# RWKV-7 units laid out by pairs of heads, with a new place for the projections of r and v, the adaLN steps and the output projection

## The chip, the cores and the metric

The kernel runs on one core of a Trainium2 chip. The metric is the device time of one execution in microseconds; of a kernel that is timed several times, the median counts. The core has engines with a queue each that run in order: TensorE (PE, with PEld for its weight loads), VectorE (DVE), ScalarE (ACT), GpSimd (POOL) and SyncE (SP), which issues most of the DMAs. Products go to PSUM, in banks that DVE and ACT read; everything else lies in SBUF, 128 partitions wide.

## What is computed

The reference is a trunk of two layers on 256 tokens of width 1024, in float32. Layer 0 is RWKV-7 time mixing and a dense SwiGLU; layer 1 is dilated attention and a mixture of experts. The change concerns the time mixing alone, 16 heads of 64 channels:

```python
def step(state, inp):
    r_t, w_t, k_t, v_t, a_t, b_t = inp
    sa = jnp.einsum('bhvk,bhk->bhv', state, a_t)
    state = state * w_t[:, :, None, :] + sa[..., None] * b_t[:, :, None, :] + v_t[..., None] * k_t[:, :, None, :]
    return state, jnp.einsum('bhvk,bhk->bhv', state, r_t)
...
_, y = lax.scan(step, s0, seq_in)
...
y = ((y - mu_y) * lax.rsqrt(var_y + LNX_EPS)).reshape(B, S, D) * lnx_g + lnx_b
bonus = (rh * kh * r_k).sum(-1, keepdims=True) * vh
y = y + bonus.reshape(B, S, D)
return (y * g).astype(h.dtype) @ w_out
...
def post_norm(t, y, l, j):
    gate = sub_mod[:, l, j, 2][:, None, :]
    return layer_norm(DEEPNORM_ALPHA * t + (1.0 + gate) * y, ln_g[l, j], ln_b[l, j])
```

r, k and v are projections of the modulated input, w, a and g come from small LoRA products, and the modulation rows (adaLN) are products of silu(c) with ada_w.

## The kernel before

**Units.** The scan is done in chunks of 64 tokens in matrix form. `unit(i, lane)` does four heads (256 channels, group `c_ = i // 2`) of 128 tokens (tile `t = i % 2`), which are two chunks `ch`. There are 8 units and 4 lanes; a lane has one PSUM tile (`psb0` to `psb3`, got with `lps`) and its own SBUF tiles, and unit i + 4 begins in the lane that is freed. A unit first makes the decayed vectors A, R (from a and r) and B, K; transposes them (ART and BKT); multiplies them to the masked scores SM; inverts a triangular matrix, E, in four doubling steps (`psb<-T,SM`, then `psb<-X,E` or, as the trace writes it, E,X) and two of 32x32; and then goes through its two chunks: products of SM with SV (which holds v and then the solved U), products of the state ST with ART, U times E, and the update of the state from SV and BKn. Y, the output of the chunk, is normalised, gated (g2t, w2t with lga, lgb) and transposed into `yg`.

**Layout.** The two halves of the partitions hold the two chunks, and the four heads lie one after the other in the free dimension. In the solve, `mm64` goes through heads and, inside, through the two halves, so neighbours alternate. The scores are made for `par = 0` and then for `par = 1`, each into the lane's tile. In the scan over chunks one half is at work at a time:

```python
for h in range(4):
    PE.matmul(ps[sl, h], E[sl, h], U[sl, h], start=True, stop=True)
```

BKn is built half by half on DVE. The update of the state is two 128x128 products, of which `pcm`, a mask with the decay in it that POOL writes, keeps the diagonal blocks.

**Order.** `spin` writes the instructions of the whole stage. Each task is a generator that yields the engine and the operands of its next step, or a condition. `spin` takes the step with the lowest pair of estimated start and order number, from a planner's clock that is part of the kernel. Units have the numbers 0 to 7. `rv_task` (number 100) makes the projections of r and v in 16 blocks of 24 matmuls; `ada_lane` (103) makes four adaLN rows of eight steps each, 512 KB of weights per step, with two buffers `rawa`; `pre_task` (104) makes the gate; `wo_task` (102) is the output projection, 96 matmuls from `yg` into the banks `mmb0` to `mmb3`, and begins when all of v, the gate and the rows are done; `pn_task` is the post-norm for each token tile, and `f0_task` the first piece of the SwiGLU. Numbers only decide between steps with the same estimate. Each engine then runs its list in order, so a step that waits holds what is listed behind it.

## Time and profile before

| | us |
|---|---|
| median of 3 runs | 1843.85 |
| lowest and highest | 1843.07, 1847.41 |
| profiled execution, own time | 1846.92 |
| profiled execution, span | 1845.2 |
| PE busy in the span | 1715.7 (93%) |
| DVE busy | 1497.0 (81%) |
| ACT busy | 1120.4 (61%) |
| POOL busy | 296.6 (16%) |

The profile is one execution; its span runs from the first to the last instruction, and its own time holds 1.7 us more. PE's share of busy time is an average over the whole trunk, most of which is the mixture of experts. The units lie between about 85 and 345 us. Below, a table by stretches gives busy time and granted clock there, groups of instructions give counts and means, and rows in order of time give the start of each run of equal instructions, its length, and in brackets how long the engine had been idle and for whom. A float32 matmul of the program shows as two in the trace.

### The profile page before, as it was taken

To read this page: it belongs to the slowest core of one execution; us is meant where nothing else is said; L and a number is where in the kernel's file an instruction comes from. 1 tells how busy PE (TensorE), PEld (TensorE's weight loads), DVE (VectorE), ACT (ScalarE), POOL (GpSimd) and SP (SyncE) were. 2 spreads that over 40 slices of the span, in tenths; PEclk is the share of its full clock that TensorE was granted. 3 is DMA by queue.
4 is the path that set the end of the run, shared out by engine and by line. 5 is a ranking of instruction groups with operands and counts; after the bars stand their busy time and mean duration, and the time that the engine had idled before them with its cause. 6 is when DMAs were issued, how large, how long until landed. Compare 5 with 4: busy or idle time off the path is not lost. (4 is left out here: it accounts for less than half of the span.)

```text
span 1845.2 us, 26366 instructions
## 1 busy us (share of the span) xinstructions
PE 1715.7 (93%) x9828; PEld 1368.3 (74%) x9828; DVE 1497.0 (81%) x2044; ACT 1120.4 (61%) x1447; POOL 296.6 (16%) x222
## 2 busy tenths in 40 slices
PE   6998998869998888979999999999999999999896
PEld 3676776558876666778888888888788787788674
DVE  2786786389886768579899898998888988988888
ACT  3443342236553656438777777877777777777674
POOL 0012222044532785250000000000000000000200
PEclk8998998889998999979999999999999999999998
DMA  9551153559894574568999999999999999999880
GB/s 330 155 160 30 54 164 116 150 189 357 296 354 151 194 256 154 195 230 293 334 352 368 357 349 380 348 360 332 345 368 340 352 345 349 352 344 359 311 320 24
DMA packets 213564, 498.94 MB, mean 270 GB/s; under 512 B 14634, under 2 KB 28818, under 8 KB 213428
## 3 DMA queue, kind: packets, MB, share of 16 engines
q1 hardware_dynamic: 212564, 494.03, 75.7%
q0 software_dynamic: 864, 3.15, 0.5%
q8 instruction: 79, 1.29, 0.3%
q14 instruction: 57, 0.47, 0.1%
HBM read 496.07 MB, written 1.06 MB: 269 GB/s over the span
## 5 line engine op out<-in xcount | busy, mean ns | idle before, releaser
L190 DVE TENSOR_TENSOR wlo<-raw,whi 128x1024 fp32r<-128x1024 f32 x800 | 991.6, 1277 | 138.0 <-ACT whi L190 123.7
L190 ACT CAST whi<-raw 128x1024 fp32r<-128x1024 f32 x808 | 823.9, 1048 | 291.9 <-PE mmb L190 221.2
L190 PE MATMUL mmb<-wlo,xeh 128*128 128x512 f32 x896 | 355.9, 397 | 5.9 <-DVE wlo L190 5.2
L190 PE MATMUL mmb<-whi,xeh 128*128 128x512 f32 x896 | 352.5, 394 | 0.0
L190 PE MATMUL mmb<-whi,xel 128*128 128x512 f32 x896 | 351.6, 392 | 0.0
L190 PEld LDWEIGHTS mmb<-wlo,xeh 128*128 128x128 f32 x896 | 168.4, 188 | 48.3 <-DVE wlo L190 14.9
L190 PEld LDWEIGHTS mmb<-whi,xeh 128*128 128x128 f32 x896 | 168.4, 188 | 34.2 <-ACT whi L190 0.2
L190 PEld LDWEIGHTS mmb<-whi,xel 128*128 128x128 f32 x896 | 168.4, 188 | 32.6
L190 PE MATMUL psb<-wlo,ah 128*128 128x512 f32 x448 | 176.7, 394 | 1.5 <-DVE wlo L190 1.5
L190 PE MATMUL psb<-whi,al 128*128 128x512 f32 x448 | 174.7, 390 | 0.0
L190 PE MATMUL psb<-whi,ah 128*128 128x512 f32 x448 | 161.8, 391 | 0.0
L190 POOL TENSOR_TENSOR macc<-macc,gate 128x1024 f32<-128x1024 f32 x2 | 5.7, 2889 | 924.8 <-ACT gate L190 924.8
L190 POOL TENSOR_TENSOR acc<-acc,raw 128x512 f32<-128x512 f32 (+1 forms) x62 | 128.2, 2082 | 74.2 <-DVE acc L190 42.9
L190 PEld LDWEIGHTS psb<-wlo,ah 128*128 128x128 f32 x448 | 84.1, 188 | 24.6 <-DVE wlo L190 6.2
L190 PEld LDWEIGHTS psb<-whi,ah 128*128 128x128 f32 x448 | 83.5, 188 | 18.8 <-ACT whi L190 1.6
L190 PEld LDWEIGHTS psb<-whi,al 128*128 128x128 f32 x448 | 84.2, 188 | 16.4
L190 PE MATMUL mmb<-whi,f_xl 128*128 128x512 f32 (+1 forms) x192 | 72.1, 375 | 1.1 <-DVE f_xl L190 1.1
L190 PE MATMUL mmb<-whi,f_xh 128*128 128x512 f32 (+1 forms) x192 | 72.7, 379 | 0.0
L190 PE MATMUL mmb<-wlo,f_xh 128*128 128x512 f32 (+1 forms) x192 | 72.0, 375 | 0.2 <-DVE wlo L190 0.2
L190 ACT CAST ah<-psb 128x512 fp32r<-128x512 f32 x56 | 32.6, 583 | 60.3 <-PE psb L190 60.2
L190 ACT ACTIVATE e_s<-mmb 128x512 f32<-128x512 f32 x56 | 33.5, 599 | 44.8 <-PE mmb L190 44.8
L190 DVE TENSOR_TENSOR e_s<-e_s,mmb 128x512 f32<-128x512 f32 x56 | 38.2, 683 | 22.5 <-PE mmb L190 22.2
(417 smaller groups left out, 2589.3 us busy)
## 6 DMA issues: line engine op xcount, KB each, us to landing
raw<-in_moe_w_gu_dram SPq DMA_DIRECT2D x192, 1024.0 KB, 6.6
raw<-in_moe_w_down_dram SPq DMA_DIRECT2D x83, 1024.0 KB, 6.1
raw<-in_moe_w_gu_dram SPq DMA_DIRECT2D x60, 512.0 KB, 7.0
raw<-in_moe_w_down_dram SPq DMA_DIRECT2D x56, 512.0 KB, 6.0
raw<-in_ada_w_dram SPq DMA_DIRECT2D x37, 512.0 KB, 5.3
rawa<-in_ada_w_dram SPq DMA_DIRECT2D x35, 512.0 KB, 4.2
raw<-in_ada_w_dram SPq DMA_DIRECT2D x15, 1024.0 KB, 7.8
raw<-in_ffn_w_gu_dram SPq DMA_DIRECT2D x21, 512.0 KB, 5.3
```

The lines of the kernel that those rows point to most:

```text
L190: return fn(*a, **kw)
```

## The change

- In the scan and the solve the halves of the partitions now hold pairs of heads (`hp`), and `ch * 2 + hh` lies in the free dimension; `each` and `products` go through both halves in turn.
- The scores of `par` 0 and 1 are issued in turn into two banks, the lane's and `mmb2`. A lock, `bank2`, lets one unit at a time into the second; the gate takes the same lock.
- B and K are built at full width (`Bf`, `Kf`, in the place of kQ) and transposed from there; BKn is filled by eight copies of 64x128 after the solve, and SV by four of 64x128 after one full memset.
- `pcm` is gone: POOL clears each new state, and DVE adds and scales the diagonal halves alone, at 64x128 each. The update of the state is four products of 64x64.
- `lgb` moves into a tile with zeros around it, and its product runs over 128 rows instead of 32.
- `rv_task` and `ada_lane` get the number 3.5; `ada_lane` takes its weight rows in pairs, both loaded before the eight matmuls of the two. `wo_task` waits in addition until all units have their masked scores (`sm_n`).
- Steps carry a hint on the shape, which has the weight zero in the planner (`SHP = 0`); the planner's estimates are otherwise as before.

```diff
-            for st in ada_pe(i, ada_raw, lambda: mmt(3), 256):
-                yield lambda: True
-                yield st
+            for q in range(0, 8, 2):
+                rws = [ada_raw(i, q + j) for j in range(2)]
+                yield PE, "128x32", rws[0], rws[1]
+                if q == 0:
+                    ps = mmt(3)
+                    PE.matmul(ps[:, 0:256], zero[:, 0:128], zero, start=True, stop=False)
+                for j in range(2):
+                    for g in range(4):
+                        PE.matmul(ps[g * 32:g * 32 + 32, 0:256], cs_act[:, q + j:q + j + 1].to_broadcast([128, 32]),
+                                  rws[j][:, g * 256:g * 256 + 256], start=False, stop=q + j == 7,
+                                  tile_position=(0, g * 32))
+            yield from ada_end(i, ps)
...
+        lgb.append(ringed("xh", 2, ap_.tile([128, S], F32, name="xh", bufs=2)))
+        yield GP,
+        GP.memset(lgb[0][:, 0:S], 0.0)
+        for dst, src in ((lga, psg), (lgb[0][96:128], psg2)):
...
+        yield V, ta, kkr
+        Bf, Kf = kkr, Q
+        V.scalar_tensor_tensor(Bf, ta, 1.0, kkr, op0=OP.add, op1=OP.mult)
+        yield V, k2, Q
+        V.tensor_tensor(Kf, k2, Q, op=OP.mult)
+
+
+        yield lambda: not bank2[0]
+        bank2[0] = 1
...
+        yield PE, "128x128", A, R, Bf, Kf
         ART = lt("ART", "ART", (128, 2, 2, 2, 64))
-        ps = lps((128, 2, 2, 2, 64))
+        BKT = lt("BKT", "BS", (128, 2, 2, 2, 64))
+        ps, psk = lps((128, 2, 2, 2, 64)), mmt(2, (128, 2, 2, 128))
...
-        yield V, kkr
-        BKn = lt("BKn", "BKn", (128, 2, 256))
-        halves(lambda sl, ch: V.scalar_tensor_tensor(BKn[sl, ch], ta[sl], 1.0, kkr[sl], op0=OP.add, op1=OP.mult))
...
+        for src, a in ((Bf, 0), (Kf, 1)):
+            for p in range(2):
+                PE.transpose(psk[:, p, a], src[:, p * 128:(p + 1) * 128], ident)
...
+        pss = [lps((128, 2, 2, 128)), mmt(2, (128, 2, 2, 128))]
+        for ch in range(2):
+            for pr in range(2):
+                for par in range(2):
+                    sl = slice(par * 64, par * 64 + 64)
+                    PE.matmul(pss[par][:, ch, pr], BKT[sl, pr, ch].rearrange("q a t -> q (a t)"),
+                              ART[sl, pr, ch].rearrange("q a t -> q (a t)"), start=True, stop=True)
...
-        for par in range(2):
-            sl = slice(par * 64, par * 64 + 64)
-            yield PE, BKT, ART
-            ps = lps((128, 2, 2, 128))
-            for ch in range(2):
-                for pr in range(2):
-                    PE.matmul(ps[:, ch, pr], BKT[sl, pr, ch, :], ART[sl, pr, ch].rearrange("q a t -> q (a t)"),
...
+        bank2[0] = 0
+        sm_n[0] += 1
...
+        def each():
+            for ch in range(2):
+                for hh in range(2):
+                    for hp in range(2):
+                        yield slice(hp * 64, hp * 64 + 64), ch, 2 * hp + hh, ch * 2 + hh
...
+        for ch in range(2):
+            for hp in range(2):
+                s_, cs_ = slice(ch * 64, ch * 64 + 64), slice(hp * 128, hp * 128 + 128)
+                for src, d in ((Bf, hp), (Kf, 1 - hp)):
+                    e = pick([SC, V], src)
+                    yield e, src
+                    (SC.copy if e is SC else V.tensor_copy)(BKn[d * 64:d * 64 + 64, ch, cs_], src[s_, cs_])
...
-        SC.copy(SV[64:128, 0], v_[0:64])
-        SC.copy(SV[0:64, 1], v_[64:128])
         yield GP,
-        GP.memset(SV[0:64, 0], 0.0)
-        GP.memset(SV[64:128, 1], 0.0)
+        GP.memset(SV.rearrange("p c n -> p (c n)"), 0.0)
+        for ch in range(2):
+            for hp in range(2):
+                s_, cs_ = slice(ch * 64, ch * 64 + 64), slice(hp * 128, hp * 128 + 128)
+                yield SC, v_, SV
+                SC.copy(SV[64 - hp * 64:128 - hp * 64, ch, cs_], v_[s_, cs_])
...
-        pcm = lt("pcm", "t34", (128, 2, 2, 128))
...
+        def products(ps, ch, a, st):
+
+            for hh in range(2):
+                for hp in range(2):
+                    h = 2 * hp + hh
+                    PE.matmul(ps[hp * 64:hp * 64 + 64, hh], SM[:, ch, h, a * 64:a * 64 + 64],
+                              SV[:, ch, h * 64:(h + 1) * 64], start=hh == 0, stop=st is None and hh == 1)
+            return ps
+
+        def with_state(ps, ch, a, st):
             for pr in range(2):
-                PE.matmul(ps[sl, 2 * pr:2 * pr + 2].rearrange("p h n -> p (h n)"), ART[:, pr, ch, a], st[:, pr],
-                          start=False, stop=pr == 1)
+                PE.matmul(ps[pr * 64:pr * 64 + 64].rearrange("p h n -> p (h n)"), ART[:, pr, ch, a], st[:, pr],
+                          start=False, stop=True)
...
+            for hh in range(2):
+                for hp in range(2):
+                    sl = slice(hp * 64, hp * 64 + 64)
+                    PE.matmul(ps[sl, hh], E[sl, ch * 2 + hh], U[sl, ch * 2 + hh], start=True, stop=True)
+            for hp in range(2):
+                sl = slice(hp * 64, hp * 64 + 64)
+                e = SC if hp else V
+                yield e, ps
+                (SC.copy if hp else V.tensor_copy)(SV[sl, ch, hp * 128:hp * 128 + 128],
...
+                ps2 = lps((128, 2, 64))
                 for pr in range(2):
-                    prs = slice(pr * 128, (pr + 1) * 128)
-                    PE.matmul(ps2[:, pr], BKn[:, ch, prs], SV[:, ch, prs], start=True, stop=True)
+                    for par in range(2):
+                        hsl = slice(pr * 128 + par * 64, pr * 128 + par * 64 + 64)
+                        PE.matmul(ps2[par * 64:par * 64 + 64, pr], BKn[:, ch, hsl], SV[:, ch, hsl], start=True,
+                                  stop=True)
                 yield V, ps2
-                sn = lt("ST", "t1", (128, 2, 128)) if ch == 0 else up.tile([128, 2, 128], F32, name=f"ST{c_ % 2}",
-                                                                                   bufs=1)
...
+                    cur = lt("Sc", "t34", (128, 2, 64))
+                    halves(lambda sl, par: V.tensor_tensor(cur[sl], ps2[sl], diag(st, sl, par), op=OP.add))
+                    yield V, cur
+                pc = PC[:, :, ch].unsqueeze(2)
+                halves(lambda sl, par: V.tensor_tensor(diag(sn, sl, par), cur[sl], pc[sl].to_broadcast([64, 2, 64]),
+                                                       op=OP.mult))
...
-            yield PE, hi, lo, xl, ps[0], ps[1]
+            yield 3.5, PE, hi, lo, xl, ps[0], ps[1]
...
-        yield lambda: len(vsb) == 8 and "gate" in pre and not ada_left[0]
+        yield lambda: len(vsb) == 8 and "gate" in pre and not ada_left[0] and sm_n[0] == 8
...
+        yield lambda: not bank2[0]
+        bank2[0] = 1
         yield from bcast_steps(2, o, lambda: mmt(2))
+        bank2[0] = 0
...
-                if isinstance(need[0], int):
+                if isinstance(need[0], (int, float)):
...
-                 (103, ada_lane(LANE)), (104, pre_task()), (105, pn_task(0)), (106, pn_task(1)),
+                 (3.5, ada_lane(LANE)), (104, pre_task()), (105, pn_task(0)), (106, pn_task(1)),
```

The order on PE where unit 3 ends and unit 4 begins; numbers tell buffers of one name apart, the figure in names such as T_4 is the unit, and mmb with x0h or x2h is a block of r or v. Before:

```order
L190 MATMUL psb_2422<-SV_3_2313,SM_3_1854 64x64 x4
L190 MATMUL psb_2422<-ST1_2050,ART_3_1399 64x128 x2
L190 MATMUL psb_2435<-sg_6_2429,cst2_112 128x256
L190 MATMUL psb_2440<-SV_3_2313,SM_3_1854 64x64 x4
L190 MATMUL psb_2440<-ST_3_2416,ART_3_1399 64x128 x2
L190 MATMUL psb_2453<-cst_79,sg_5_2139 128x128 x2
L190 MATMUL psb_2453<-cst_79,P_5_2176 128x128 x2
L190 MATMUL psb_2462<-T_4_2450,SM_4_2364 64x64 x8
L190 MATMUL psb_2475<-U_3_2318,E_3_1937 64x64 x4
L190 MATMUL mmb_2353<-whi_2207,x0h_254 128x256
```

And after:

```order
L191 MATMUL mmb_2613<-rawa_2569,cs_act_96 32x256 x4
L191 MATMUL mmb_2613<-rawa_2571,cs_act_96 32x256 x4
L191 MATMUL psb_2646<-U_3_2487,E_3_1764 64x64 x4
L191 MATMUL psb_2655<-cst_79,sg_4_2102 128x128 x2
L191 MATMUL psb_2655<-cst_79,P_4_2148 128x128 x2
L191 MATMUL mmb_2656<-cst_79,kQ_4_2086 128x128 x4
L191 MATMUL psb_2671<-SV_3_2457,SM_3_1655 64x64 x4
L191 MATMUL psb_2671<-ST_3_2489,ART_3_1618 64x128 x2
L191 MATMUL psb_2681<-w2t_265,lw_267 128x256
L191 MATMUL psb_2681<-a2t_266,la_268 128x256
L191 MATMUL psb_2695<-ART_4_2653,BKT_4_2654 128x128
L191 MATMUL mmb_2696<-ART_4_2653,BKT_4_2654 128x128
```

Before, unit 4 is in its solve while a block of r begins; after, unit 4's scores (ART_4, BKT_4) alternate between two tiles, all blocks of r and v stand ahead of this piece, and adaLN steps come in pairs.

The order on PE at the end of unit 7 (mmb with ygh or ygl is the output projection, cst with Y_7 the transposes of the unit's result). Before:

```order
L190 MATMUL mmb_3698<-rawa_3837,cs_act_96 32x256 x4
L190 MATMUL mmb_3698<-rawa_3860,cs_act_96 32x256 x4
L190 MATMUL mmb_3698<-cst_79,row_3892 128x128 x2
L190 MATMUL mmb_3901<-whi_2666,ygh_1125 128x512
L190 MATMUL mmb_3901<-wlo_2667,ygh_1125 128x512
L190 MATMUL mmb_3901<-whi_2666,ygl_1126 128x512
L190 MATMUL psb_3910<-g2t_868,lga_269 128x256
L190 MATMUL psb_3910<-w2t_265,lw_267 128x256
L190 MATMUL mmb_3902<-whi_2666,ygh_1125 128x512
L190 MATMUL mmb_3902<-wlo_2667,ygh_1125 128x512
L190 MATMUL mmb_3902<-whi_2666,ygl_1126 128x512
L190 MATMUL psb_3917<-cst_79,Y_7_3763 128x128 x2
```

And after:

```order
L191 MATMUL psb_4114<-U_7_4019,E_7_3695 64x64 x4
L191 MATMUL mmb_3690<-whi_4048,ygh_1087 128x512
L191 MATMUL mmb_3690<-wlo_4049,ygh_1087 128x512
L191 MATMUL mmb_3690<-whi_4048,ygl_1088 128x512
L191 MATMUL mmb_3690<-whi_4071,ygh_1087 128x512
L191 MATMUL mmb_3690<-wlo_4072,ygh_1087 128x512
L191 MATMUL mmb_3690<-whi_4071,ygl_1088 128x512
L191 MATMUL psb_4128<-SV_7_4013,SM_7_3615 64x64 x4
L191 MATMUL psb_4128<-ST_7_4021,ART_7_3589 64x128 x2
L191 MATMUL psb_4168<-g2t_864,lga_269 128x256
L191 MATMUL psb_4168<-w2t_265,xh_775 128x256
L191 MATMUL psb_4178<-cst_79,Y_7_4020 128x128 x2
```

Before, the projection begins behind the last adaLN step, with six of its matmuls ahead of Y_7; after, it lies between the links of unit 7, and 84 of its 96 matmuls stand ahead of Y_7.

The order on ACT from the last products of unit 7's solve to its first chunk. Before:

```order
L190 COPY X_7_3660<-psb_3646 128x256
L190 COPY row_3677<-mmb_3253 128x256
L190 ACTIVATE ysq_6_3679<-Y_6_3520 128x256
L190 COPY X_7_3702<-psb_3703 32x4x32 x2
L190 COPY gate1_3699<-mmb_3725 128x512
L190 COPY SV_7_3757<-vsb1_2781 64x256 x2
L190 CAST ygh_1125<-psb_3774 128x2x128
L190 COPY U_7_3762<-psb_3768 64x256
L190 COPY SV_7_3757<-psb_3788 64x256
L190 COPY gate1_3699<-mmb_3800 128x512
```

And after:

```order
L191 COPY X_7_3934<-psb_3916 128x256
L191 CAST whi_3957<-raw_3880 128x1024
L191 COPY X_7_3962<-psb_3963 32x4x32 x2
L191 COPY BKn_7_3694<-kQ_7_2886 64x128 x8
L191 COPY SV_7_4013<-vsb1_2820 64x128 x4
L191 CAST ygh_1087<-psb_4032 128x2x128
L191 COPY U_7_4019<-psb_4027 128x128
L191 CAST whi_4048<-raw_3929 128x1024
L191 COPY SV_7_4013<-psb_4040 64x128
L191 CAST whi_4071<-raw_3982 128x1024
```

Before, two copies fill SV_7 ahead of U_7; after, eight to BKn_7 and four to SV_7 stand there, and casts of the projection's weights (whi) lie between the unit's copies.

## Rows read from the trace of the kernel before

**Rows 1.** Stretches: length, busy us of the engines (instructions), granted clock, DMA, GB/s.

```profile
85.00:159.00 74.00, 67.10 (x837) 55.80 (x835) 61.36 (x174) 31.23 (x77) 12.31 (x21) 1.00 0.41 123
159.00:204.00 45.00, 40.25 (x416) 31.62 (x416) 27.09 (x101) 13.94 (x38) 9.83 (x16) 0.74 0.03 8
204.00:250.00 46.00, 43.04 (x506) 35.91 (x504) 36.79 (x100) 19.63 (x47) 13.61 (x21) 1.00 0.43 136
250.00:295.00 45.00, 39.66 (x581) 29.10 (x577) 37.68 (x133) 16.38 (x47) 10.02 (x18) 1.00 0.41 129
295.00:339.00 44.00, 36.52 (x439) 24.81 (x439) 17.41 (x62) 11.68 (x31) 6.95 (x12) 0.81 0.49 144
```

**Rows 2.** Groups on PE, 85 to 339: shape, count, busy us, mean, idle before.

```profile
L190 PE MATMUL psb<-SV,SM 128*64 128x64 f32 x256 | 23.4, 240 | 4.8 <-DVE ST L190 2.2 <-DVE E L190 1.0 <-DVE bon L190 0.9
L190 PE MATMUL mmb<-rawa,cs_act 128*32 128x256 f32 x256 | 21.8, 419 | 4.8 <-DMA rawa<-in_ada_w_dram 4.8
...
L190 PE MATMUL psb<-ART,BKT 64*128 64x128 f32 x128 | 18.4, 284 | 3.1 <-DVE yna L190 2.3 <-ACT BKT L190 0.7
L190 PE MATMUL psb<-ST,ART 128*64 128x128 f32 x96 | 15.2, 283 | 0.0
...
L190 PE MATMUL psb<-U,E 64*64 64x64 f32 x128 | 11.9, 240 | 0.0
L190 PE MATMUL psb<-SV,BKn 128*128 128x128 f32 x48 | 10.0, 339 | 0.0
```

**Rows 3.** PE in order of time, three places: start, us, what, count.

```profile
121.71 1.16 PE L190 MATMUL psb<-ART,BKT 64*128 64x128 f32 x8
122.80 0.68 PE L190 MATMUL psb<-E,X 64*64 64x64 f32 x16
...
150.83 0.68 PE L190 MATMUL psb<-E,X 64*64 64x64 f32 x16
151.44 0.71 PE L190 MATMUL psb<-SV,BKn 128*128 128x128 f32 x4
152.08 0.68 PE L190 MATMUL psb<-E,X 64*64 64x64 f32 x16
152.84 0.68 PE L190 MATMUL psb<-SV,SM 128*64 128x64 f32 x8
153.36 0.60 PE L190 MATMUL psb<-ST,ART 128*64 128x128 f32 x4
153.89 0.82 PE L190 MATMUL psb<-T,SM 32*32 32x32 f32 x24
...
322.92 0.67 PE L190 MATMUL psb<-U,E 64*64 64x64 f32 x8
323.53 0.64 PE L190 MATMUL mmb<-rawa,cs_act 128*32 128x256 f32 x8
324.10 1.16 PE L190 MATMUL mmb<-cst,mod 128*128 128x128 f32 x8
```

**Rows 4.** Groups on ACT and DVE, 85 to 345.

```profile
L190 ACT COPY SV<-vsb 64x256 f32<-64x256 f32 x16 | 6.4, 403 | 0.4
...
L190 ACT COPY X<-psb 32x128 f32<-32x128 f32 x16 | 4.1, 258 | 9.4 <-PE psb L190 9.1
...
L190 DVE SCALAR_TENSOR_TENSOR BKn<-ta,kQ 64x256 f32<-64x256 f32 x16 | 6.8, 423 | 0.1
```

**Rows 5.** PE in order of time, end of the stage.

```profile
334.54 0.64 PE L190 MATMUL mmb<-rawa,cs_act 128*32 128x256 f32 x8 [2.16 <-DMA rawa<-in_ada_w_dram]
...
339.10 0.78 PE L190 MATMUL mmb<-whi,ygh 128*128 128x512 f32 x1
...
344.11 0.63 PE L190 MATMUL psb<-cst,Y 128*128 128x128 f32 x2
...
378.27 1.11 PE L190 MATMUL psb<-cst,u 128*128 128x128 f32 x4 [9.43 <-DVE u L190]
```

**Rows 6.** The page's DMA issues: count, KB each, median us to landing.

```profile
rawa<-in_ada_w_dram SPq DMA_DIRECT2D x35, 512.0 KB, 4.2
```

More of the change, by code (lines that the diff above doesn't have):

```diff
@@ L1039, in unit @@
             SC.copy(X, ps)
-            yield PE, X
+            yield PE, "64x64", X
             ps = lps((128, 4, 64))
-            mm64(ps, lambda sl, ch, h: X[sl, h], lambda sl, ch, h: E[sl, h])
+            for sl, ch, h, j in each():
+                PE.matmul(ps[sl, j], X[sl, j], E[sl, j], start=True, stop=True)
             yield V, ps
@@ L1101, in unit @@
-            first = t == 0 and ch == 0
-            yield PE, SV
-            ps = lps((128, 4, 64))
-            for h in range(4):
-                PE.matmul(ps[sl, h], SM[:, ch, h, 0:64], SV[:, ch, h * 64:(h + 1) * 64], start=h == 0,
-                          stop=first and h == 3)
+            first, final = t == 0 and ch == 0, t == 1 and ch == 1
+            if not final:
+                sn = lt("ST", "t1", (128, 2, 128)) if ch == 0 else up.tile([128, 2, 128], F32, name=f"ST{c_ % 2}",
+                                                                           bufs=1)
+                yield GP,
+                GP.memset(sn.rearrange("p r n -> p (r n)"), 0.0)
@@ L1110, in unit @@
                 st = ST[c_]
-                yield PE, st
-                with_state(ps, sl, ch, 0, st)
-            yield SC, ps
-            SC.copy(U[sl], ps[sl])
-            yield PE, U
-            ps = lps((128, 4, 64))
-            for h in range(4):
-                PE.matmul(ps[sl, h], E[sl, h], U[sl, h], start=True, stop=True)
-            yield SC, ps
-            SC.copy(h4(SV[sl, ch]), ps[sl])
-            if not (t == 1 and ch == 1):
-                yield PE, SV
-                ps2 = lps((128, 2, 128))
+            yield PE, "128x64", SV
@@ L1134, in unit @@
                 ST[c_] = sn
                 ST_n[c_] = t * 2 + ch + 1
-            yield PE, SV
-            ps = lps((128, 4, 64))
-            for h in range(4):
-                PE.matmul(ps[sl, h], SM[:, ch, h, 64:128], SV[:, ch, h * 64:(h + 1) * 64], start=h == 0,
-                          stop=first and h == 3)
+            yield PE, "128x64", SV
+            ps = lps((128, 2, 64))
+            products(ps, ch, 1, st)
             if not first:
-                with_state(ps, sl, ch, 1, st)
@@ L1143, in unit @@
[L1143 to L1144 removed]
+                with_state(ps, ch, 1, st)
+            for hp in range(2):
+                yield SC, ps
+                SC.copy(Y[ch * 64:ch * 64 + 64, 2 * hp:2 * hp + 2], ps[hp * 64:hp * 64 + 64])
         yield GP, v_, bon
```

114 lines of the change are left out of this document (60 added, 54 removed).

## The prediction

> **What bounds the kernel now.** I read the stage table first [rows 1], because the change touches only the RWKV-7 stage and the start of the output projection, about 85 to 380 us of a span of 1845.2 us. The reader is to see three things. PE is busy 67.10 of 74 us, then 40.25 of 45, 43.04 of 46, 39.66 of 45 and 36.52 of 44: it is the fullest engine, but no stretch is solid, and DVE has 61.36 of 74 us in the first, so a faster PE would soon meet DVE there. The granted clock is 1.00 in three stretches and only 0.74 and 0.81 in the second and the last, where almost nothing but units runs; those two are mixtures of 1.2 and 2.4 GHz. In the last stretch ACT (11.68) and DVE (17.41) are nearly idle and PE still has gaps: what ends last there is the chain of the last two units. Then I read the groups on PE by shape, for counts [rows 2], and the order of time, for the price from one run's start to the next [rows 3]; the mean of a matmul in a group is longer than its price, since matmuls overlap. Last I read the end of the stage [rows 5]: the first matmul of the output projection stands at 339.10, the last unit's transposes (Y) at 344.11, and the first product of the post-norm (u) at 378.27, after 9.43 us without any PE work. So 34.2 us lie between the last unit and the next stage, in which the projection has no company.
>
> **PE work taken away.** A matmul of the program is two in the trace, so a run of four is x8. The new layout issues neighbours that lie in different halves of the array, where the old one issued them in the same half.
> - Masked scores (ART,BKT): 128 in the groups are 16 runs, 1.09 us each (121.71 to 122.80) [rows 2, 3], 17.4 us. Alternating halves, at best half: -8.7. That a row half runs beside the other is shown for 64-column products: 16 of E,X, which alternate, take 0.61 us (150.83 to 151.44), as long as 8 of U,E, which don't (322.92 to 323.53).
> - Products (SV,SM): 256 are 32 runs of 0.52 us, 16.6 us; they now alternate between column halves: -8.3. Column groups are shown by rawa: 8 matmuls of 256 columns in four groups take 0.57 us (323.53 to 324.10), 71 ns each, where one of 128 columns with the state takes 0.53/4 = 133 ns.
> - With the state (ST,ART): 96 are 24 runs of 0.53 us (153.36 to 153.89), 12.7 us, also in column halves: -6.4.
> - U,E: 16 runs of 0.61 us, now like E,X: -4.9.
> - State update (SV,BKn): 48 are 12 runs of 0.64 us (151.44 to 152.08). Four 64-wide ones in column halves cost half a run of SV,SM, 0.26: 12 x 0.38 = -4.6; without any company they cost 0.52, -1.4.
> The sum is -32.9 us if every pair shares the array and -1.4 if none does; I take -31, because both kinds of sharing stand in the rows, though not with 128 columns. The transposes of B and K read the full-width tiles and are as many as before, and the LoRA product over 128 rows instead of 32 has as many columns: nothing for both.
> Half of the 31 falls on units 0 to 3. PE is busy 107.35 of 119 us up to 204, but DVE has 61.36 of 74 in the first stretch, which covers part: I take **-12** of 15.5 (bounds -5 and -15.5). On units 4 to 7 PE is busy 119.2 of 135 us, with the projections of r and v as filler that now goes ahead (the order at unit 4: before, a block of r follows unit 4's first solve product; after, all blocks stand ahead of its scores). These four blocks change place, not amount: nothing in the sum. With less filler the chain counts, not PE: **-6** of 15.5 (bounds 0 and -14).
>
> **The end of the stage.** In the order of before, the projection stands behind the last adaLN row, and only that lies ahead of the last unit's tail. After, it begins behind unit 7's scores, and 84 of its 96 matmuls stand ahead of unit 7's Y. The last 12 cost about 3 us by a pace of (368.85 - 344.11)/(96 - 6) = 0.27 us, where 368.85 is 378.27 less the idle 9.43 [rows 5], and 6 stand ahead of Y in the order of before. The two banks of the first token tile are complete before Y, so the post-norm's first part doesn't wait for the last unit. Y to u becomes 3 + 9.4 = 12.4 us instead of 34.2: **-22**. The price is that 84 matmuls, 19 to 24 us of PE, go between the links of units 6 and 7. Their cover is the idle 7.48 us of 295 to 339, some 8 us freed there by the layout, and the place of 13 adaLN steps (13 x 0.57 = 7.4 us) that leave this stretch. That is 23 us: just enough, so this term can lose up to all of it (bounds -28, with a shorter 9.4, and 0). Its weights' casts go to ACT and DVE, busy 11.68 and 17.41 of 44 us there: nothing.
>
> **What is added.**
> - adaLN in pairs. Both rows are now loaded after the pair before has freed both buffers, and PE, which runs in order, waits with all units' products behind it when the second is late. A load takes 4.2 us [rows 6]. Before, all single steps together waited 4.8 us, the longest 2.16 us [rows 2, 5]. Some 10 pairs follow unit 4's start. Between -5 (the late steps vanish since they come earlier) and +21 (all ten wait 2.1 us) I take **+5**, nearer to the rows of single steps, since most of those didn't wait.
> - Narrow copies on a unit's path. After the solve ACT has eight copies of 64x128 to BKn and four to SV, where it had two of 64x256. Twelve at 258 ns (the nearest small copy, 32x128) are 3.1 us, at 403 ns (64x256) 4.8 us, less 0.8 [rows 4]. The third excerpt shows them in a row ahead of unit 7's U. Per unit +2.3 to +4.0, two generations of units in a lane, other lanes' work fills part: **+4** (bounds 0 and +8). On DVE the four 64x256 steps of 423 ns that built BKn per unit become two of full width: a small gain off the path.
> - The guard on the second bank of the scores: a unit that reaches its scores waits for the other's masks. Only two or three units are ever near; in the sum of the next point.
> - Clock and queues. Without the filler, 204 to 295 may be granted as 159 to 204 was (0.74 instead of 1.00). If PE were the bound, 82.7 us of work would grow by a third; with the chain as bound it costs only the links' own PE time. I take **+4** (bounds 0 and +12).
> Sum: -12 - 6 - 22 + 5 + 4 + 4 = **-27 us**. The profiled execution's own time is 1846.92 us, 1.72 over its span, so 1819.9 on its scale; the median is 3.07 us lower, so 1816.8, **1817 us**. What follows the stage moves as a whole: from 400 us on I assume that it keeps its length.
>
> **A rule against the rows.** E,X alternates between row halves and writes one bank, and still runs twice as fast as U,E [rows 3]. The Trainium skill, TensorEngine Tiling (Array Packing), Restrictions and Gotchas, says that different row tiles cannot access the same PSUM bank at once. By that rule U,E would gain nothing (the scores go to two banks) and the sum would be 2 to 3 us smaller; the trace's 0.61 us for 16 speaks against it.
>
> **Rivals.**
> 1. *The freed PE time isn't felt* (0.17): the chain of a unit bounds everywhere, or halves don't share the array with wide operands. Against it stand 107.35 of 119 us of PE. Then -18 becomes -4: -13, **1831 us**. The rule above, as a case of its own in which U,E alone keeps its length, has 0.02 and gives **1820 us**.
> 2. *The projection isn't hidden* (0.10), so the change doesn't do what its order says: the 84 matmuls fall on PE when units 6 and 7 need it, or their weights come late, and Y moves by what is saved behind it. For it: the cover was just enough. -22 becomes -3: -8, **1836 us**.
> 3. *All of it is felt* (0.19): PE gives -25, the projection -26, and the additions cost 8: -43, **1801 us**. For it: PE is the fullest engine in all five stretches.
> 4. *Slower* (0.06): the pairs. When each of ten pairs stalls PE for a whole load, 4.2 us, all lanes stop together: +42 instead of +5 gives +10, **1854 us**. It decides from 3.2 us per pair on (then the sum is zero). Against it: the longest wait of a step is 2.16 us, and the planner spaces the pairs.
>
> **How the numbers follow.** The forecast, 1807 to 1827 us, has 0.46. The range of 1799 to 1838 us takes in rivals 1, 2 and more than half of 3, and leaves out rival 4 and the far end of 3. About 0.3% (5.5 us) is what a measurement can tell from no change. Faster: 0.46 + 0.17 + 0.02 + 0.19 and a third of rival 2, 0.87; the same: most of the rest of 2, 0.06; slower: rival 4 and its neighbourhood, 0.07.
>
> **What would show it.** In the profile after: runs of eight scores near 1.1 us that were two of 1.09; products in 0.26; unit 4's scores with no r or v product behind them; u about 12 us behind unit 7's Y, and Y itself some 5 us earlier than 344.11. It is wrong if the alternating runs keep their length (rival 1), if Y comes later than 360 with projection matmuls between the links (rival 2), if PE shows waits of 3 us and more for rawa (rival 4), or if the stages behind 400 us change in length.

## The result, and the profile after

The changed kernel takes 1827.76 us (median of 4 runs, 1827.28 to 1830.45) where the kernel before takes 1844.26 (4 runs); the ratio is 0.9900, with a 95% interval of 0.9881 to 0.9918. The forecast was 1817 us, in a range of 1799 to 1838: the sign and the range held, the gain was 16.5 us instead of 27.

Stretches of the profile after, as in [rows 1]: length, busy us of PE, PEld, DVE, ACT, POOL (instructions), granted clock, DMA share, GB/s.

```profile
85.00:159.00 74.00, 65.21 (x925) 55.45 (x926) 59.01 (x179) 34.83 (x99) 10.51 (x17) 0.99 0.45 137
159.00:204.00 45.00, 41.83 (x571) 34.64 (x569) 26.82 (x78) 20.03 (x54) 7.28 (x13) 0.94 0.40 136
204.00:250.00 46.00, 36.87 (x458) 23.44 (x454) 42.14 (x154) 19.08 (x61) 9.57 (x13) 0.89 0.51 171
250.00:295.00 45.00, 36.76 (x599) 27.47 (x598) 31.90 (x112) 23.38 (x80) 7.80 (x15) 0.87 0.32 106
295.00:339.00 44.00, 38.65 (x383) 26.74 (x382) 28.14 (x80) 18.62 (x44) 5.75 (x8) 0.97 0.29 85
```

The reader should see two things. Between 204 and 295 PE has 36.87 and 36.76 us of work where it had 43.04 and 39.66, and is granted 0.89 and 0.87 of its clock where it had 1.00. And DVE is now busy 42.14 of 46 us from 204 on.

The groups on PE that answer to [rows 2], 85 to 339 (of the scores, those into the second bank; as many go into the lane's):

```profile
L191 PE MATMUL mmb<-rawa,cs_act 128*32 128x256 f32 x256 | 20.1, 432 | 0.4 <-DMA rawa<-in_ada_w_dram 0.4
...
L191 PE MATMUL psb<-SV,SM 128*64 128x64 f32 x256 | 17.1, 247 | 8.6 <-ACT SV L191 3.5 <-DVE ST L191 2.1 <-ACT Y L191 1.9
...
L191 PE MATMUL psb<-ST,ART 128*64 128x128 f32 x96 | 11.0, 302 | 0.0
L191 PE MATMUL mmb<-ART,BKT 64*128 64x128 f32 x64 | 9.9, 299 | 0.0
L191 PE MATMUL psb<-U,E 64*64 64x64 f32 x128 | 7.6, 242 | 1.2 <-ACT U L191 1.0
...
L191 PE MATMUL psb<-SV,BKn 128*64 128x64 f32 x96 | 5.9, 250 | 1.7 <-ACT SV L191 1.7
```

And PE in order of time, for prices (as [rows 3]) and for the end of the stage (as [rows 5]): start, length, what, count, idle before.

```profile
323.54 0.45 PE L191 MATMUL psb<-U,E 64*64 64x64 f32 x8 [0.37 <-ACT U L191]
323.92 0.51 PE L191 MATMUL mmb<-whi,ygh 128*128 128x512 f32 x1
...
326.91 0.45 PE L191 MATMUL psb<-SV,BKn 128*64 128x64 f32 x8
327.29 0.50 PE L191 MATMUL mmb<-whi,ygh 128*128 128x512 f32 x1
...
328.88 0.45 PE L191 MATMUL psb<-SV,SM 128*64 128x64 f32 x8
329.16 0.39 PE L191 MATMUL psb<-ST,ART 128*64 128x128 f32 x4
...
330.47 0.39 PE L191 MATMUL psb<-ST,ART 128*64 128x128 f32 x4
330.79 0.50 PE L191 MATMUL mmb<-whi,ygh 128*128 128x512 f32 x1
...
344.48 0.69 PE L191 MATMUL psb<-cst,Y 128*128 128x128 f32 x2 [8.39 <-DVE Y L191]
...
351.16 1.37 PE L191 MATMUL psb<-cst,u 128*128 128x128 f32 x8
...
367.18 1.11 PE L191 MATMUL psb<-cst,u 128*128 128x128 f32 x4 [3.28 <-DVE u L191]
```

Prices first. Eight matmuls of U,E take 0.38 us (323.54 to 323.92) instead of 0.61, the state update 0.38 (326.91 to 327.29) instead of 0.64, the products 0.28 (328.88 to 329.16) instead of 0.52, those with the state 0.32 (330.47 to 330.79) instead of 0.53. All sums of PE time from one start to the next between 85 and 344 us, at full clock and without idle time, give 71 ns a score (135 before), 45 ns a product (66), 85 with the state (134), 46 for U,E (74), and 4.7 us for twelve state updates at 49 ns a matmul in the place of 7.5 (156 ns). Times their counts (128, 256, 96, 128) that is 8.2 + 5.4 + 4.7 + 3.6 + 2.8 = **24.7 us** that the layout takes off PE.

Then the end. The last unit's transposes (Y) stand at 344.48, where they stood at 344.11. The first product of the post-norm (u) follows at 351.16, 6.7 us behind, where it was 34.2; the second token tile's at 367.18. From 395 to 600 us every event of the trace lies 20.4 us before its twin, and 21.3 us in the mixture of experts. So the whole gain sits behind Y, and the units gave none. These are single executions: the two profiled ones lie 19.6 us apart, the medians 16.5, because the profiled execution of the kernel before is 2.7 us above its median.

In the post-norm DVE and POOL get in each other's way. DVE and then POOL, in order of time:

```profile
344.35 0.68 DVE L191 SCALAR_TENSOR_TENSOR u<-xres,u 128x512 f32<-128x512 f32 x1
...
351.82 2.33 DVE L191 SCALAR_TENSOR_TENSOR u<-xres,u 128x512 f32<-128x512 f32 x1
...
355.94 0.67 DVE L191 TENSOR_TENSOR u<-mmb,gate 128x512 f32<-128x512 f32 x1
356.53 2.68 DVE L191 TENSOR_TENSOR f_xl<-modtmp,f_xh 128x512 fp32r<-128x512 f32 x1
359.14 2.90 DVE L191 SCALAR_TENSOR_TENSOR u<-xres,u 128x512 f32<-128x512 f32 x1
...
351.24 5.11 POOL L191 TENSOR_TENSOR wlo<-rawa,whi 128x1024 fp32r<-128x1024 f32 x2 [8.03 <-ACT whi L191]
356.31 2.35 POOL L191 TENSOR_TENSOR u<-u,gb 128x1024 f32<-128x1024 f32 x1
358.74 2.74 POOL L191 TENSOR_TENSOR xres<-u,bb 128x1024 f32<-128x1024 f32 x1
```

A step of DVE with two operands in SBUF takes 0.68 us alone (344.35) and 2.33, 2.68 and 2.90 us beside a tensor step of POOL (351.82, 356.53, 359.14). The last two end 0.55 us behind the POOL step beside which they began (359.21 behind 358.66, 362.04 behind 361.48), as if they had waited for it. A step with one operand in PSUM (355.94, u from mmb and gate) keeps its 0.67 us beside the same POOL step.

### The profile page after: what moved, and what is told of

It reads as the page before. It is cut to its first block, busy times and chain, and to the rows that moved or that the text cites. A ratio compares the mean times of both kernels' runs of the same rounds, so it can differ in the third digit from the quotient of the medians.

```text
span 1825.5 us, 26566 instructions
## 1 busy us (share of the span) xinstructions
PE 1687.7 (92%) x9876; PEld 1341.9 (74%) x9876; DVE 1499.5 (82%) x2072; ACT 1136.4 (62%) x1542; POOL 287.9 (16%) x205
## 5 line engine op out<-in xcount | busy, mean ns | idle before, releaser
L191 DVE TENSOR_TENSOR wlo<-raw,whi 128x1024 fp32r<-128x1024 f32 (+1 forms) x799 | 990.3, 1277 | 141.5 <-ACT whi L191 127.4
L191 PEld LDWEIGHTS psb<-wlo,ah 128*128 128x128 f32 x448 | 84.1, 188 | 24.7 <-DVE wlo L191 6.2
```

Of the source, the lines that this page charges most:

```text
L191: return fn(*a, **kw)
```

## The experiments

Each kernel is compared with the kernel before in the same job, whose median was 1844.3 to 1848.5 us there, so that ratios compare better than microseconds. "Y" and "u" are the last unit's transposes and the first product of the post-norm in the kernel's profile, which is one execution.

### What the layout does without the new order

The four places where the changed kernel sets the order, put back as before (the pairs' loop, of which the head stands here, goes as a whole):

```diff
-                 (3.5, ada_lane(LANE)), (104, pre_task()), (105, pn_task(0)), (106, pn_task(1)),
+                 (103, ada_lane(LANE)), (104, pre_task()), (105, pn_task(0)), (106, pn_task(1)),
-            yield 3.5, PE, hi, lo, xl, ps[0], ps[1]
+            yield PE, hi, lo, xl, ps[0], ps[1]
-            for q in range(0, 8, 2):
-                rws = [ada_raw(i, q + j) for j in range(2)]
-                yield PE, "128x32", rws[0], rws[1]
...
+            for st in ada_pe(i, ada_raw, lambda: mmt(3), 256):
+                yield lambda: True
+                yield st
-        yield lambda: len(vsb) == 8 and "gate" in pre and not ada_left[0] and sm_n[0] == 8
+        yield lambda: len(vsb) == 8 and "gate" in pre and not ada_left[0]
```

> The new layout with the order rules of before: r and v at number 100, single adaLN steps at 103, the projection without the condition on the scores. Theory PE (the units go as fast as PE has time, and what the new order puts ahead of unit 7 used up the 25 us that the products give back): unit 7's Y comes 18 to 25 us before 344, the rest behind it stays, 1820 to 1827 us. Theory chain (a unit's links on DVE and ACT set the pace, PE's freed time isn't felt): Y stays within 4 us of 344, 1840 to 1848 us.

Measured: 1821.63 us, ratio 0.9884 (0.9848 to 0.9921). The end of the stage on PE, the last adaLN step, the first projection matmul, Y and u:

```profile
293.27 0.64 PE L191 MATMUL mmb<-rawa,cs_act 128*32 128x256 f32 x8
...
295.51 0.48 PE L191 MATMUL mmb<-whi,ygh 128*128 128x512 f32 x1
...
335.32 0.69 PE L191 MATMUL psb<-cst,Y 128*128 128x128 f32 x2 [8.39 <-DVE Y L191]
...
341.62 1.11 PE L191 MATMUL psb<-cst,u 128*128 128x128 f32 x8 [0.23 <-DVE u L191]
```

Y comes 8.8 us before 344.11, a part of what theory PE wanted. The surprise is the second row: with the old rules the projection begins at 295.51, 40 us ahead of Y, and u follows 6.3 us behind it. The overlap that the prediction put down to the new order comes with the layout alone: the projection waits for the last adaLN step, and with the layout's other steps in its list the planner puts that at 293.27, where in the kernel before one still stood at 334.54 [rows 5]. By the times alone this kernel and the changed one can't be told apart (the intervals overlap); by their profiles, one execution each, it is 8.4 us ahead in the mixture of experts (29.7 before the twin events of the kernel before, against 21.3).

### What the new order does without the layout

The reverse: the kernel before, with the four new rules and no new layout.

```diff
-                 (103, ada_lane(LANE)), (104, pre_task()), (105, pn_task(0)), (106, pn_task(1)),
+                 (3.5, ada_lane(LANE)), (104, pre_task()), (105, pn_task(0)), (106, pn_task(1)),
-            yield PE, hi, lo, xl, ps[0], ps[1]
+            yield 3.5, PE, hi, lo, xl, ps[0], ps[1]
-            for st in ada_pe(i, ada_raw, lambda: mmt(3), 256):
+            for q in range(0, 8, 2):
+                rws = [ada_raw(i, q + j) for j in range(2)]
...
-        yield lambda: len(vsb) == 8 and "gate" in pre and not ada_left[0]
+        yield lambda: len(vsb) == 8 and "gate" in pre and not ada_left[0] and sm_n[0] == 8
```

> The old layout with the new order rules: r, v and adaLN at 3.5, adaLN in pairs, the projection from the last scores on. Theory PE: 84 projection matmuls lie ahead of Y with nothing freed for them, Y some 20 us later, u 22 us nearer to it, 1838 to 1846 us. Theory chain: the matmuls fall into gaps, Y stays, the end is 20 us nearer, 1822 to 1829 us.

Measured: 1850.62 us, ratio 1.0025 (1.0006 to 1.0044). Unit 7's first scores in the kernel before and in this one, then the same three events:

```profile
286.73 1.16 PE L190 MATMUL psb<-ART,BKT 64*128 64x128 f32 x8 [0.68 <-ACT BKT L190]
...
310.33 2.08 PE L190 MATMUL psb<-ART,BKT 64*128 64x128 f32 x8
...
324.12 0.50 PE L190 MATMUL mmb<-whi,ygh 128*128 128x512 f32 x1
...
369.61 0.69 PE L190 MATMUL psb<-cst,Y 128*128 128x128 f32 x2 [6.01 <-DVE Y L190]
...
375.92 1.11 PE L190 MATMUL psb<-cst,u 128*128 128x128 f32 x8
```

Y comes 25.5 us later and u 2.4 us earlier. The projection is indeed moved ahead of Y (84 matmuls), but that isn't what makes Y late: unit 7's scores stand at 310.33 where they stood at 286.73 in the kernel before, 23.6 us later, and the projection begins behind them. So the delay comes with the other rules, early r and v and the adaLN pairs; which of them isn't shown. The new rules alone lose a little, and the time lies above both ranges.

### The projection behind the units

```diff
-        yield lambda: len(vsb) == 8 and "gate" in pre and not ada_left[0] and sm_n[0] == 8
+        yield lambda: len(vsb) == 8 and "gate" in pre and not ada_left[0] and done.get((2, 3), 0) == 2
```

> The changed kernel, but the output projection waits until the last unit's result is normalised, so all 96 matmuls stand behind the units. Theory PE: the units 4 to 7 get PE back and Y comes 15 to 20 us before 344, the projection then takes 25 us alone: 1828 to 1836 us. Theory chain: Y stays at 340 to 345, the 25 us come on top: 1847 to 1853 us.

Measured: 1839.61 us, ratio 0.9963 (0.9942 to 0.9984). One stretch, then Y:

```profile
295.00:339.00 44.00, 31.95 (x331) 23.70 (x328) 23.83 (x89) 11.71 (x38) 5.66 (x9) 0.62 0.00 1
...
340.41 0.38 PE L191 MATMUL psb<-cst,Y 128*128 128x128 f32 x2
```

The edit did less than was expected of it: the last steps of unit 7's result are on DVE, and 27 projection matmuls (7.4 us, from 333.05 on) still stand ahead of Y in PE's list. The changed kernel has 84 there (24.6 us). With 17.2 us of PE gone from ahead of it, Y comes only 4.1 us earlier, where theory chain had it; the time lies between the two ranges. Unit 7's scores, ahead of which the lists are the same, came 2.8 us later in this execution (289.84 instead of 287.07), so from there to Y the gain is 6.9 us. The row shows what came with it: the engine that had filler to 38.65 of 44 us at a clock of 0.97 now has 31.95 at 0.62. That the lower clock is what held Y back is a reading; no run holds the clock fixed. This part of the overlap is worth some 12 us, by the difference of the medians.

### POOL away from the post-norm

```diff
-            e = pick([V, GP], f0raw[q], o[0]) if q < F0V else GP
+            e = pick([V, GP], f0raw[q], o[0]) if q < 2 else V
-        yield lambda: len(f0) == 4
+        yield lambda: len(f0) == 4 and fxn[1] == 2
-    WH, BG0, F0V = 1, 0, 2
+    WH, BG0, F0V = 1, 0, 4
```

> The changed kernel with POOL kept off the post-norm: the low parts of the first SwiGLU weights on DVE, and the residual of token tile 0 only after tile 1 is modulated. In the trace four DVE steps of 0.42 to 0.69 us took 2.33 to 2.90 us while POOL ran such a tensor step. If this overlap is what stretches them and they lie on the path, the second token tile's u comes 4 to 8 us earlier and the time is 1819 to 1824 us. Rival: what follows waits for weights or PE anyway, 1826 to 1829 us.

Measured: 1825.85 us, ratio 0.9900 (0.9862 to 0.9937). The steps that were stretched, DVE and then POOL, and Y on PE:

```profile
354.99 0.69 DVE L191 SCALAR_TENSOR_TENSOR u<-xres,u 128x512 f32<-128x512 f32 x1
...
356.73 0.69 DVE L191 TENSOR_TENSOR f_xl<-modtmp,f_xh 128x512 fp32r<-128x512 f32 x1
...
360.12 2.90 DVE L191 TENSOR_TENSOR f_xl<-modtmp,f_xh 128x512 fp32r<-128x512 f32 x1
...
354.20 5.45 POOL L191 TENSOR_TENSOR u<-u,gb 128x1024 f32<-128x1024 f32 x1 [8.84 <-PE psb L191]
359.73 2.74 POOL L191 TENSOR_TENSOR xres<-u,bb 128x1024 f32<-128x1024 f32 x1
...
346.63 0.69 PE L191 MATMUL psb<-cst,Y 128*128 128x128 f32 x2 [8.39 <-DVE Y L191]
```

With the casts on DVE, the steps at 354.99 and 356.73 are back at 0.69 us. The second edit did nothing on the chip: POOL's residual step still runs beside DVE from 354.20. This time DVE's steps keep their length and POOL's takes 5.45 us instead of 2.35; the next POOL step, from 359.73, stretches the DVE step at 360.12 to 2.90. From Y to the first transposes of the SwiGLU it is 45.9 us instead of 50.9 (single executions, from the start of Y). The ratio is that of the changed kernel, so the times don't resolve the gain.

This run shows something else: up to Y every engine's list is that of the changed kernel, and yet Y came 2.1 us later and unit 7's scores 3.1 (290.21). Some 45 us up to Y were granted the lower clock, where it was 37.3. A shift of Y by 2 us between two single profiles is therefore no proof that an edit did it.

The same edit on top of the old rules, so the first kernel above with these lines, has the lowest time here:

```diff
-        yield lambda: len(f0) == 4
+        yield lambda: len(f0) == 4 and fxn[1] == 2
-            e = pick([V, GP], f0raw[q], o[0]) if q < F0V else GP
+            e = pick([V, GP], f0raw[q], o[0]) if q < 2 else V
```

> The new layout, the order rules of before, and the post-norm without POOL as in e4: low parts of the first SwiGLU weights on DVE, the residual of tile 0 behind tile 1's modulation. If what e4 took off the way from Y to the SwiGLU (5.0 us in the profiles) adds to what the old rules gain, 1815 to 1819 us. Rival: the old rules put other work there and POOL isn't in the way, 1820 to 1823 us.

Measured: 1817.13 us, ratio 0.9837 (0.9815 to 0.9859), in the range expected, 6 parts in a thousand below the changed kernel and clear of its interval, but not of the interval of the layout with the old rules. Its Y and u stand where they do in the kernel with the old rules alone (335.23 and 341.54); in the mixture of experts its profile lies 33.1 us ahead of the kernel before, where that one was 29.7.

### Is PE's freed time felt? Two runs with the order held fixed

In these runs the planner counts the same steps as in the changed kernel, so every engine's list is the same but for the edit. In the first, the scores, the products, U,E and the state updates are issued one half after the other; the diff has the scores, and the three others are changed alike.

```diff
+        for par in range(2):
+            for ch in range(2):
+                for pr in range(2):
+                    score(nc.tensor, par, ch, pr)
-                    PE.matmul(pss[par][:, ch, pr], BKT[sl, pr, ch].rearrange("q a t -> q (a t)"),
-                              ART[sl, pr, ch].rearrange("q a t -> q (a t)"), start=True, stop=True)
```

> The changed kernel with the order of every engine as it is, but within a run of scores, products, U,E and state updates one half of the array follows the other instead of alternating: the sharing of the array is lost for the scores and halved for the others, some 12 to 15 us of PE more. If the units feel PE's time, unit 7's Y comes 8 to 15 us after 344.5 and the time is 1834 to 1843 us. If their chain or the other engines set the pace, Y moves by less than 5 us, 1826 to 1832 us.

Measured: 1829.74 us, ratio 0.9906 (0.9887 to 0.9925). One run of scores, first half and second half (eight each), what follows it, and Y:

```profile
104.80 0.82 PE L1029 MATMUL psb<-ART,BKT 64*128 64x128 f32 x5
...
105.79 0.72 PE L1029 MATMUL mmb<-ART,BKT 64*128 64x128 f32 x5
106.44 1.13 PE L192 MATMUL psb<-sg,cst 128*128 128x256 f32 x4
...
346.40 0.69 PE L192 MATMUL psb<-cst,Y 128*128 128x128 f32 x2 [8.39 <-DVE Y L192]
```

The expectation had the size of the edit wrong. Only the scores became dearer: 16 take 1.64 us (104.80 to 106.44) where the same run of the changed kernel took 1.09, and summed over all runs it is 103 ns instead of 71 at full clock, 4.1 us in all; products and U,E cost 45 and 47 ns as before, though two in one half now stand ahead of two in the other. Y moved by 1.9 us, no more than the 2.1 us by which two profiles of one list differed above, and the ratio isn't clear of the changed kernel's. Whether the 4.1 us were felt stays open.

In the second, three quarters of the last group's r and v products are counted by the planner and not issued:

```diff
+                    mute[0] = c_ == 3 and kk not in (0, 7)
                     mm3(ps[t], xh[:, kk, tsl], ...)
+                    mute[0] = False
```

> The changed kernel in the same order, but of the four late blocks of r and v (channel group 3) only 6 of 24 matmuls each are made, so the projections of that group leave out three quarters of their sum: 8.6 us of PE less between 185 and 202. Theory blocks (they hold the scans of units 2 and 3 and the front of unit 4): unit 4's scores come 6 to 9 us before 224.7, Y follows, 1819 to 1823 us. Rival (units 4 to 7 are set by DVE behind 204): scores move by less than 3 us, 1825 to 1829 us.

Measured: 1823.14 us, ratio 0.9867 (0.9851 to 0.9884). Y:

```profile
341.24 0.69 PE L192 MATMUL psb<-cst,Y 128*128 128x128 f32 x2 [8.39 <-DVE Y L192]
```

8.6 us of PE less between 185 and 202 bring unit 4's scores 3.6 us forward, Y 3.2 and everything behind 400 us 4.0, with two or three us of doubt for a pair of single profiles; by the ratios it is 6 us. So about half was felt there. The scores lie between the two theories, the time at the upper end for theory blocks. Part of what was saved went to the clock: some 52 us up to Y were granted the lower one, where it was 37.3.

### The narrow copies

Each copy to BKn is issued a second time, behind the planner's back:

```diff
                     (SC.copy if e is SC else V.tensor_copy)(BKn[...], src[s_, cs_])
+                    (nc.scalar.copy if e is SC else nc.vector.tensor_copy)(BKn[...], src[s_, cs_])
```

> The changed kernel in the same order, each of the eight BKn copies of a unit made twice: 8 x 0.27 = 2.2 us more per unit on ACT, between the solve and U. Theory path (they lie on a unit's chain, and two units follow each other in a lane): Y 3 to 5 us later, 1830 to 1834 us. Rival (other lanes' work covers them): within 2 us of 1827.8.

Measured: 1850.11 us, ratio 1.0008 (0.9997 to 1.0020). Groups on ACT, 85 to 345, the copies made a second time and the first time, and Y:

```profile
L1117 ACT COPY BKn<-kQ 64x128 f32<-64x128 f32 x61 | 18.1, 296 | 1.9
L191 ACT COPY BKn<-kQ 64x128 f32<-64x128 f32 x61 | 18.0, 295 | 0.6
...
365.55 0.69 PE L191 MATMUL psb<-cst,Y 128*128 128x128 f32 x2 [8.39 <-DVE Y L191]
```

18.1 us of copies on ACT, an engine that is busy 116 of 260 us there, put Y back by 21.1 us and take the whole gain of the change. That is more than the 2.2 us per unit that I allowed, nearly five times what the two units of a lane add up to. ACT runs its list in order, so the eight copies of one unit also hold what the three others have listed behind them, and PE waits: its idle time up to Y that ended with ACT's copies to SV grew from 5.2 to 17.8 us. Of the time from 85 us to Y, 72.9 us were granted the lower clock of 1.2 GHz, against 37.3 in the changed kernel.

Putting the copies elsewhere didn't help. On top of the fastest kernel, the same block moved from behind the solve to where BKn is made:

```diff
+        for ch in range(2):
+            for hp in range(2):
+                s_, cs_ = slice(ch * 64, ch * 64 + 64), slice(hp * 128, hp * 128 + 128)
+                for src, d in ((Bf, hp), (Kf, 1 - hp)):
+                    e = pick([SC, V], src)
+                    yield e, src
+                    (SC.copy if e is SC else V.tensor_copy)(BKn[d * 64:d * 64 + 64, ch, cs_], src[s_, cs_])
```

> As e8_layout_tail, with the eight BKn copies right behind the masked scores, ahead of the solve. Theory path (these 2.2 us per unit lie between the solve and U): Y 2 to 5 us earlier, 1811 to 1816 us. Rival: ACT's eight copies now stand ahead of the solve's X of all lanes and cost the same there, within 2 us of e8_layout_tail.

Measured: 1845.11 us, ratio 0.9985 (0.9970 to 0.9999), 28 us above its base. adaLN matmuls on PE, the last ahead of a hole and the first behind it:

```profile
235.70 1.08 PE L191 MATMUL mmb<-rawa,cs_act 128*32 128x256 f32 x8
...
286.76 1.08 PE L191 MATMUL mmb<-rawa,cs_act 128*32 128x256 f32 x8
```

No adaLN step ran for 50 us, the gate came late, and the projection began at 334.7. I took SP for the cause, where the load of bb waited between, and gave the rows gb and bb to POOL's queue, behind the adaLN rows:

```diff
+        yield lambda: not ada_left[0]
         for nm, tag, src in (("gb", "ksb0", ln_g), ("bb", "ksb1", ln_b)):
             pre[nm] = up.tile([128, D], F32, name=nm, tag=tag, bufs=1)
+            by_gp.add(pre[nm].tensor.name)
             bcast_row(pre[nm], src[0, 0])
```

> As e9_layout_tail_early, but the two rows of the post-norm (gb and bb) are loaded by POOL's queue behind the gate instead of by SP's. In e9 the load of bb waited on SP until unit 7 had read k, and no adaLN row was issued between 239 and 288. Theory SP queue: the rows come without that hole, the projection starts before 300, 1812 to 1820 us. Rival (the planner's order, which put unit 7's front late, is what costs): 1838 to 1846 us.

Measured: 1847.40 us, ratio 1.0005 (0.9988 to 1.0022). The same two steps:

```profile
234.44 1.08 PE L191 MATMUL mmb<-rawa,cs_act 128*32 128x256 f32 x8
...
288.63 1.08 PE L191 MATMUL mmb<-rawa,cs_act 128*32 128x256 f32 x8
```

The hole is still there, with bb off SP's queue, so that theory falls. The order itself shows what is left: the weights of the step at 288.63 were asked for by 236, and PE works through the scores of units 5 and 6 (242.62 and 251.97) and their solves in between, so its list has no adaLN step from there to the front of unit 7. The planner laid it out so once the copies had moved; why it did isn't shown.

### One rule at a time

The changed kernel with single adaLN steps:

```diff
-            for q in range(0, 8, 2):
-                rws = [ada_raw(i, q + j) for j in range(2)]
...
+            for st in ada_pe(i, ada_raw, lambda: mmt(3), 256):
+                yield lambda: True
+                yield st
```

> The changed kernel with single adaLN steps, one row ahead, still at number 3.5 as are r and v. Theory blocks (the four late blocks of r and v, 11.4 us of PE in a stretch in which the units' scans run, keep DVE and ACT idle and then leave them 10 us behind): the pairs cost nothing, unit 4's scores stay within 4 us of 224.7, 1825 to 1831 us. Theory pairs (16 matmuls in a row and the later loads are what delays the units): scores and Y some 8 us earlier, 1818 to 1823 us.

Measured: 1847.16 us, ratio 0.9989 (0.9971 to 1.0008).

And with the last blocks of r and v at their old rank:

```diff
-            yield 3.5, PE, hi, lo, xl, ps[0], ps[1]
+            yield PE, hi, lo, xl, ps[0], ps[1]
```

> The changed kernel with r and v back at number 100, adaLN still in pairs at 3.5. Theory blocks: the last four blocks go to where units 4 to 7 leave gaps, unit 4's scores come 8 to 12 us before 224.7, Y before 338, 1818 to 1823 us. Theory pairs: scores and Y stay within 3 us, 1825 to 1831 us.

Measured: 1845.41 us, ratio 0.9978 (0.9962 to 0.9994). Both theories miss by 20 us: with either rule undone alone Y is at 368.7 and 368.6 (the second profile is the slowest of its ten executions), with both rules in place it is at 344.5, and with none of the new rules at 335.3. A stretch of the kernel with single adaLN steps:

```profile
250.00:295.00 45.00, 37.59 (x594) 29.82 (x595) 26.69 (x89) 18.45 (x62) 3.55 (x8) 0.67 0.20 60
```

DVE (26.69 of 45 us) and ACT (18.45) are half idle, and the clock is 0.67. The two kernels' lists differ from the changed kernel's on every engine from the first step that the planner weighs anew, so these runs don't price a rule. What in those lists costs the 24 us stays open.

## Why the prediction was right, and where it was wrong

- **PE work taken away: 31 us forecast, 24.7 measured.** The mechanism was right in all five forms. U,E gives 3.6 of 4.9 and the scores 8.2 of 8.7; the products were taken at half of 0.52 and cost 0.28 only where those with the state follow (328.88 to 329.16), 0.36 on average, so 5.4 instead of 8.3. The case of the rule, that U,E keeps its length, is refuted: 0.38 us instead of 0.61, with both halves in one bank. There the Trainium skill (TensorEngine Tiling (Array Packing), Restrictions and Gotchas) says that different row tiles cannot access one PSUM bank at once, and the measurement decides. The two halves write different partitions of the bank here (0 to 63 and 64 to 127); halves that write the same partitions were not tried.
- **"-12 and -6": the units give nothing in the changed kernel.** Y is at 344.48; with the additions (+5, +4, +4) the sum had it 5 us earlier. Where the order was held fixed, 8.6 us less in one place gave 3 to 6, and 4.1 us more over all scores can't be told from nothing. By the first, 24.7 us would be worth some 9 to 17, a rough estimate; I had 18 of 31. So the step that failed is the account of the units as a whole: what PE gave was used up, and which addition used how much stays open. Layout alone moved Y by 8.8.
- **"-22" for the end of the stage: 27.5 between Y and u, but 20.4 at 400 us.** The step was right that the idle 24 us of the projection go, and that the post-norm no longer waits. It overlooked what is late next: the second tile's u, which DVE reaches behind the steps that POOL stretched, comes 16.0 us behind the first, where it came 5.9 behind in before (384.21 less 378.27). It was wrong about whose merit it is: the overlap comes with the layout alone, and with the new rules alone it comes too, but then Y is late.
- **"Nothing" for the four late blocks of r and v.** In the changed kernel they stand between the scans of units 2 and 3, where PE is busy 17.77 of 18 us from 186 to 204 and DVE 7.21; of DVE's waits there PE ended 5.7 us and ACT's casts of weights 5.2. Cutting 8.6 of their 11.4 us gave 4.0, so they aren't free there. What they cost at their old place no run shows, so that the price of the move stays open.
- **"+5" for the adaLN pairs: 0.4 us of waits.** The row is in the groups above (4.8 before); the profile of the POOL experiment, with the same lists, has 2.9. The slower rival, in which PE stalls for loads, did not come.
- **"+4" for the narrow copies was worked out in the wrong way.** I priced the path of one unit. A second set of the same copies cost 21.1 us at Y, because they hold other units' copies too. What the first set costs isn't shown, since the changed kernel without it was not run; a second set need not cost what the first does. It is one likely place of what units 0 to 7 did not give.
- **"+4" for clock and queues:** the time at the lower clock did not grow, 37.3 us up to Y and 45.6 before; between 204 and 295 it did, as feared, but 159 to 204 and 295 to 339 rose from 0.74 and 0.81 to 0.94 and 0.97. The fear had a ground, though: 72 to 73 us in the runs with the projection last and with copies twice.

So the time was inside the range since one large term, the end of the stage, was right: -22 forecast, 20.8 from Y to 400 us. That it came out so near is in part luck, since Y to u gave 27.5 and the delay of the second tile, which the forecast hadn't seen, took 7 back. Ahead of Y the sum was -18 + 13 = -5 and nothing came. There the errors did not cancel: too much from PE and the wrong account of the copies both made the forecast too low, and only the pairs, taken too dear, made up for some of it. The range held because it was drawn to take in the first rival. Of the rivals, the first (1831 us) is nearest to 1827.76 and is right that Y would hardly move, but not in its reason: the halves share the array, and PE's time was felt where 8.6 us were cut.

## What to carry to other kernels

When several dependent chains share engines that run in order, price an added step by everything that is queued behind it on its engine, in all chains, and not by the one chain it belongs to. Before crediting a change of order with a gain, hold the lists fixed and change one cost: where a planner lays out the order anew, undoing one rule is another program. And when a fuller engine is relieved, ask what its clock does: 17.2 us of work taken from ahead of the last unit moved it by 4 us only, while its clock fell from 0.97 to 0.62. And before a shift of two us between profiles is called an effect, see how far two profiles of one list lie apart.

## What was not expected of the hardware

- TensorE ran products in alternating column halves of 128x64 at 45 ns each where 66 was the price in one half, and two in one half followed by two in the other at the same 45; four and four cost 103 ns for the scores where alternating cost 71. This fits a half that begins before the other half's short run has ended; two and two was not tried for the scores.
- A DVE step with two SBUF operands took 2.33 to 2.90 us instead of 0.68 when a tensor step of POOL was already running; where DVE's steps kept their 0.69, POOL's took 5.45 instead of 2.35. DVE steps with an operand in PSUM kept 0.67 beside POOL. The Trainium skill (GPSIMD Engine Reference, Key points) says that GpSimd shares its SBUF interfaces with VectorE and contends with DVE instructions that have two SBUF inputs; the rows agree.
